# Helper loads in program order, two tile sets per phase for the kept sums, and a unit's additions written ahead of its low part

## The chip, the cores and the metric

The kernel runs on one core of one Trainium2 chip. The metric is the device time of one execution in microseconds (us). Before the change it is 2220.44 us, the median of three runs (2217.88 to 2223.58). The execution that the hardware profiler recorded took 2220.94 us.

## The reference, cut to what matters

Two residual layers on one sequence of 256 tokens with 2048 channels, all in float32. Layer 0 mixes tokens by attention in a neighbourhood of a grid, layer 1 by a short gated convolution; each is followed by a gated MLP of width 5632 with a three-tap convolution after its up-projection; a last RMS norm closes.

```python
for i in range(DEPTH):                                  # DEPTH = 2
    a = rms_norm(h, mix_norm[i])
    mixed = neighborhood_attention(a, ...) if i == 0 else short_conv_mixer(a, ...)
    h = h + mixed
    h = h + conv_glu_ffn(rms_norm(h, ffn_norm[i]), ...)  # dwconv3(W_up x)+b, silu(g)*u, W_down
return rms_norm(h, final_norm)
```

With 256 tokens every weight is used once, so the program is a stream of weights: some 486 MB are read from HBM, split, multiplied and forgotten.

## The kernel before, in words

**Two roundings of one weight.** Weights arrive in float32. A piece of 128 x 1024 (a *chunk*) is loaded into a tile `raw` by the SP queue (six such tiles in turn, `RAWS`). ScalarE (ACT in the profile) casts it to the matmul's format, `hi` (L179), and VectorE (DVE) subtracts to get what the cast lost, `lo` (L180). TensorE (PE) multiplies by both, so each chunk costs ACT one cast and DVE one subtraction beside the matmuls. `prep_to` emits loads, casts and subtractions; it runs `AHEAD` = 4 entries of the list of chunks ahead of the item whose matmuls are being emitted.

**Stages.** `Phase` computes a product whose result has channels on the partitions: query/key (four groups of heads), the short convolution's input (`wsc`), the MLP's up-projection (`wup`, each layer in two halves, here *up 00, 01, 10, 11*). An item is two output blocks of 128 channels: 4 chunks, 32 matmuls with `hi` (L251) and 32 with `lo` (L259). When an item's `lo` matmuls end, its results are taken out of PSUM: `corr` on ACT and on DVE (L304, L305), then for the MLP a multiplication into `pad` (L310), a convolution (L318 on ACT, twice L320 on DVE), a gate (L724, L727) and a split (L283 on ACT, L284 on DVE). For query and key it is L304, L305, L574, L283, L284, and then the scores (L596 to L598 on PE), the bias (L603), the maximum (L606), the exponential (L608), L609, L611, and transposes on PE (L621). `Values` computes the values after each query/key group. `Tokens` computes a product whose result has tokens on the partitions: `wo`, the MLP's down-projection (`wdown`, *down 00 to 11*) and `wscout`.

**Seven products in the place of eight.** In `Tokens` a plan (`S_MLP`, `S_ATT`, `S_OUT`) names pairs of blocks of inner channels; a pair marked H (a *kept unit*) is computed with seven block products, which need sums of weight blocks. Two of the sums are made early, by a *job*: `make` loads three 128 x 512 pieces into tiles of the pool of activations (`act`, SP queue, L192), adds on DVE (L198, L199) and stores two results to DRAM through the ACT queue (L204, tile `kept`). The jobs are spread over the phases that stand ahead of the stage that needs them (`QK_JOBS`, `V_JOBS`, `UP_JOBS`, `SC_JOBS`); in the list of chunks a job is an entry of its own, `"make"`, placed by `Phase.__init__` between items `lo` and `hi` of the phase. Its additions are emitted when four, and its stores when seven, further entries have been prepared. In the kept unit the stored sums come back as one `raw` (t13), are split, and two additions on DVE (L159, L160) make the two other sums (t24), which are split too.

**Who sets the order.** The program is written for a scheduler: instructions are emitted in the order of the code, the scheduler puts each on its engine's queue when it reckons its inputs to be there, and `tc.issue_after` keeps an instruction behind another. What comes out is a fixed list for each engine, worked off from the top: an instruction that waits holds up all behind it on its engine. The loads of a job's pieces stand behind the newest load (`newest["SP"]`), but the loads of chunks carry no such order among themselves or against the jobs.

Of the kernel before, what the change touches and what calls it, by code (L numbers as in the profile page):

```python
# [15 lines left out]
F32 = mybir.dt.float32  # L16
F32R = mybir.dt.float32r
# [5 lines left out]
P = 128  # L23
D = 2048
S = 256
KT = D // P
# [8 lines left out]
CH = 8  # L35
# [10 lines left out]
def plan(text, due):  # L46


    words = text.split()
    return (tuple(int(x[1:]) for x in words), {int(x[1:]) for x in words if x[0] == "H"}, due)  # L50
# [5 lines left out]
         (1, 0): S_FIRST, (1, 1): (plan("P0 P2 H1 H3 H4 P9 H6 H7 H8 P5 P10", 1), plan("P0 P2 H1 H3 P5 H4 H6 H7 P8 P9 P10", 0))}  # L56
S_OUT = (plan("P0 H1 H2 P3 H4 H5 H7 P6", 0), plan("P0 P3 H1 H2 H4 H5 H7 P6", 0))
S_ATT = (plan("P0 P1 P2 H6 P3 H7 P4 P5", 1),) * 2
QK_JOBS, V_JOBS, UP_JOBS, SC_JOBS = (0, 4, 4, 0), (2, 3, 2, 0), (9, 8, 11, 8), 16


HEAD = (2, 4)
# [9 lines left out]
C_END = C_ID + P  # L72

LEAD = 96
RAWS = 6


@with_exitstack
def trunk(ctx, tc, xT, par, bias, wqk, wv, wo, wsc, wscout, wup, wdown, out):
    nc = tc.nc  # L80
    cp = ctx.enter_context(tc.tile_pool(name="const", bufs=1))
    wp = ctx.enter_context(tc.tile_pool(name="wts", bufs=1))
# [8 lines left out]

    cp.tile([P, LEAD], F32, name="lead")
    pt = cp.tile([P, C_END], F32, name="pt")
# [31 lines left out]
    prepped = []  # L125

    stores = []

    def prep_to(n):
        while len(prepped) < min(n, len(chunks)):  # L130
            src, w, kind = chunks[len(prepped)]
            for due in [x for x in stores if x[0] <= len(prepped)]:
                stores.remove(due)
                due[1]()
            if kind == "make":
                make(*src)
                prepped.append(())
                continue
            raw = wp.tile([P, CH * P], F32, name="raw", tag="raw", bufs=RAWS)
            if kind == "rows":  # L140
                newest["SP"] = nc.sync.dma_start(out=raw[:, :w], in_=src)
                prepped.append(parts(raw[:, :w]) + (raw,))
                continue

            if kind == "kept":
                newest["SP"] = nc.sync.dma_start(out=raw, in_=src())
                t13 = parts(raw)
                prepped.append((t13, parts(pair_of_sums(raw, prepped[-1][2], prepped[-2][2]))))
                continue

            newest["SP"] = nc.sync.dma_start(out=raw[:, :4 * w].rearrange("p (f c) -> p f c", f=4),
                                             in_=src.rearrange("f p c -> p f c"))
            prepped.append(parts(raw[:, :4 * w].rearrange("p (f k c) -> p f k c", f=4, c=P)) + (raw,))

    def pair_of_sums(t13, w22, left):

        l = left.rearrange("p (f k c) -> p k f c", f=4, c=P)
        t2, t4 = w22[:, :4 * P], w22[:, 4 * P:].rearrange("p (f c) -> p f c", f=4)
        nc.vector.tensor_add(out=t2, in0=t13[:, :4 * P], in1=t2)  # L159
        nc.vector.tensor_add(out=t4, in0=t2.rearrange("p (f c) -> p f c", f=4), in1=l[:, 1])  # L160
        return w22

    def parts(r):

        if len(r.shape) == 4 and r.shape[2] == 1:
            y = wp.tile([P, CH * P], F32R, name="hi", tag="hi", bufs=6)
            hi, lo = y[:, :4 * P], y[:, 4 * P:]
            return split_parts(hi, lo, r)
        hi = wp.tile([P, CH * P], F32R, name="hi", tag="hi", bufs=6)
        lo = wp.tile([P, CH * P], F32R, name="lo", tag="lo", bufs=6)  # L170
        return split_parts(hi, lo, r)

    def split_parts(hi, lo, r):
# [5 lines left out]
        newest["ACT"] = nc.scalar.copy(out=hv, in_=r)  # L179
        newest["DVE"] = nc.vector.tensor_sub(out=lv, in0=r, in1=hv.bitcast(F32))  # L180
        return hi, lo

    kept, newest = {}, {}

    def make(w, g, i):

        kept[id(w), g, i] = dst = dp.tile([P, 8 * P], F32, name=f"kept{len(kept)}")
        tiles = [act_tile().bitcast(F32) for _ in range(3)]
        for x, f, k in zip(tiles, (0, 4, 4), (0, 0, 1)):
            f, k = 8 * g + f, 2 * i + k  # L190
            with tc.issue_after(newest["SP"].ins):
                nc.sync.dma_start(out=x.rearrange("p (f c) -> p f c", f=4),  # L192
                                  in_=w[f:f + 4, :, k * P:(k + 1) * P].rearrange("f p c -> p f c"))
        l, r, t = tiles

        def adds():
            with tc.issue_after(newest["DVE"].ins):
                nc.vector.tensor_add(out=l, in0=l, in1=r)  # L198
                nc.vector.tensor_add(out=t, in0=t, in1=r)  # L199

        def store():
            for n, x in enumerate((l, t)):
                with tc.issue_after(newest["ACT"].ins):
                    nc.scalar.dma_start(out=dst[:, n * 4 * P:(n + 1) * 4 * P], in_=x)  # L204
        stores.append((len(prepped) + 4, adds))
        stores.append((len(prepped) + 7, store))

    jobs = []

# [1 line left out]
        jobs.extend((w, g, i) for g, (order, sset, _) in enumerate(plans) for i in order if i in sset)  # L211

    def take(n):
        out, jobs[:] = jobs[:n], jobs[n:]
        return out

    class Phase:

        def __init__(self, w, fts, nk, src, evac, intro=0, step=CH, jobs=()):
# [73 lines left out]
    def act_tile():  # L295
        return ap_.tile([P, 2 * S], F32R, name="act", tag="act", bufs=HALF)
# [259 lines left out]
    a2 = [None] * KT  # L556
# [289 lines left out]
    Phase(wsc, range(3 * KT), KT, a2, sc_evac, intro=3, jobs=take(SC_JOBS))  # L846
    Tokens(wscout, KT, yT, to_norm(3, a3), S_OUT, yforms)
    mlp(1, a3, last_evac())

# [33 lines left out]
    for r in range(KT // STEP):  # L883
        for i in range(STEP // 2):
            k = r * STEP + 2 * i
# [97 lines left out]
```

## Time and profile before

| | |
|---|---|
| profiled execution | 2220.94 us, span 2219.1 us |
| granted TensorE clock, mean | 0.997 |
| busy time of PE / DVE / ACT | 2190.1 / 1853.0 / 1290.4 us |
| attention (query/key, values, scores) | 0 to 305 us |
| `wo` | 305 to 394 us |
| up 00, down 00 | 394 to 641, 641 to 755 us |
| up 01, down 01 | 755 to 998, 998 to 1118 us |
| short convolution's input, `wscout` | 1118 to 1392, 1392 to 1483 us |
| up 10, down 10 | 1483 to 1730, 1730 to 1847 us |
| up 11, down 11 and the end | 1847 to 2091, 2091 to 2219 us |

A row of the list of groups reads: line, engine, operation, written tile and read tiles, shapes, number; then busy time, mean nanoseconds of one, and the engine's idle time ahead of them with what ended most of it. A row of the timeline reads: start, length, engine, line, operation, tiles, number of instructions joined in the row, and in brackets the idle time ahead of it and its releaser. Matmuls are pipelined, so their cost is read from start to start.

### The profile page before, as it was taken

How to read it: one execution, taken by the hardware profiler on the slowest of the kernel's cores; microseconds unless marked ns; L12 is line 12 of the kernel's file. 1: busy time of each engine (PE TensorE's matmuls, PEld its weight loads, DVE VectorE, ACT ScalarE, POOL GpSimd, SP SyncE). 2: the span in 40 equal slices, each digit the busy share in tenths (PEclk: the TensorE clock that was granted, in tenths of full speed). 3: DMA queues.
4: the chain of work that ended last, by engine and by line, in shares of the span. 5: the costliest groups of instructions: out<-in, count | busy, mean ns of one | idle time of the engine just before them, and what ended most of it. 6: DMA issues, size and time to landing. Idle time of an engine off the chain costs nothing.

```text
span 2219.1 us, 33057 instructions
## 1 busy us (share of the span) xinstructions
PE 2190.1 (99%) x11710; PEld 1887.3 (85%) x11710; DVE 1853.0 (84%) x2856; ACT 1290.4 (58%) x1991; POOL 109.0 (5%) x159
## 2 busy tenths in 40 slices
PE   9999999999999999999999999999999999999998
PEld 8888888888888888887888888878888878888886
DVE  8788778888889888788887777888788989888888
ACT  7555555666665666565564455566556556566565
POOL 1011100000000000000000010000010000000000
PEclk9999999999999999999999999999999999999999
DMA  8799647777657788766698885677876667877575
GB/s 290 252 323 296 209 158 222 259 249 248 213 185 231 232 264 256 237 198 208 211 321 283 275 273 190 198 242 252 265 248 212 199 226 248 251 249 237 160 234 157
DMA packets 347670, 524.91 MB, mean 237 GB/s; under 512 B 19824, under 2 KB 250352, under 8 KB 347504
## 3 DMA queue, kind: packets, MB, share of 16 engines
q1 hardware_dynamic: 327120, 487.55, 68.9%
q10 hardware_dynamic: 20384, 35.24, 4.2%
q8 instruction: 92, 1.51, 0.3%
q14 instruction: 74, 0.61, 0.1%
HBM read 486.01 MB, written 36.70 MB: 236 GB/s over the span
## 4 chain that ended last, share of the span: by engine, by line
PE 73%; DVE 15%; issue 5%; ACT 3%; DMA 3%; SPq 0%; POOL 0%; ACTq 0%; DVEq 0%
PE mm L251 36%; PE mm L259 19%; DVE lo L180 7%; PE mm L444 3%; PE mm L443 3%; PE mm L442 3%; ACT hi L179 3%; DVE raw L160 1%; PE mm L668 1%; PE mm L670 1%; PE mm L669 1%; DVE raw L159 1%; DVE hi L180 1%; DMA act<-in_wdown 1%; DMA raw<-in_wup 1%
## 5 line engine op out<-in xcount | busy, mean ns | idle before, releaser
L180 DVE TENSOR_TENSOR lo<-raw,hi 128x1024 fp32r<-128x1024 f32 (+1 forms) x858 | 1020.3, 1214 | 121.4 <-ACT hi L179 70.7
L179 ACT CAST hi<-raw 128x1024 fp32r<-128x1024 f32 (+1 forms) x924 | 905.1, 1009 | 371.7 <-DVE raw L160 136.2
L251 PE MATMUL mm<-a,hi 128*128 128x512 f32 x4096 | 962.9, 391 | 2.0 <-DVE a L292 0.9
L251 PEld LDWEIGHTS mm<-a,hi 128*128 128x128 f32 x4096 | 759.7, 188 | 156.0 <-DVE a L292 2.2
L259 PEld LDWEIGHTS mm<-a,lo 128*128 128x128 f32 x4096 | 513.8, 192 | 14.2 <-DVE lo L180 2.4
L259 PE MATMUL mm<-a,lo 128*128 128x256 f32 x4096 | 519.9, 283 | 2.2 <-DVE lo L180 2.2
L442 PE MATMUL mm<-hi,act 128*128 128x512 f32 x624 | 245.0, 394 | 5.3 <-DVE h L339 2.1
L444 PE MATMUL mm<-hi,act 128*128 128x512 f32 x624 | 243.8, 391 | 0.0
L318 ACT ACTIVATE conv<-pad,pt 128x256 f32<-128x256 f32 x176 | 103.0, 599 | 207.7 <-DVE pad L310 199.5
L443 PE MATMUL mm<-lo,act 128*128 128x512 f32 x564 | 220.5, 391 | 0.0
L320 DVE SCALAR_TENSOR_TENSOR conv<-pad,pt,conv 128x256 f32<-128x256 f32 x384 | 178.3, 480 | 27.3 <-ACT conv L318 20.7
L304 ACT COPY corr<-mm 128x256 f32<-128x256 f32 x256 | 90.9, 370 | 159.6 <-PE mm L259 138.1
L442 PEld LDWEIGHTS mm<-hi,act 128*128 128x128 f32 x624 | 117.6, 188 | 33.2 <-ACT hi L179 5.0
L444 PEld LDWEIGHTS mm<-hi,act 128*128 128x128 f32 x624 | 117.4, 188 | 24.3
L443 PEld LDWEIGHTS mm<-lo,act 128*128 128x128 f32 x564 | 106.4, 189 | 22.1
L305 DVE TENSOR_TENSOR corr<-mm,corr 128x256 f32<-128x256 f32 x256 | 104.7, 417 | 10.4 <-ACT corr L304 10.2
L198 DVE TENSOR_TENSOR act<-act 128x512 f32<-128x512 f32 x66 | 45.9, 695 | 67.2 <-DMA act<-in_wdown 45.2
L284 DVE TENSOR_TENSOR act<-conv,act 128x256 fp32r<-128x256 f32 x88 | 40.1, 456 | 61.0 <-ACT act L283 61.0
L442 PE MATMUL mu<-hi,sf 128*128 128x512 f32 x186 | 73.5, 395 | 7.3 <-ACT hi L179 7.3
L443 PE MATMUL mu<-lo,sf 128*128 128x512 f32 x186 | 73.4, 395 | 1.1 <-DVE lo L180 1.1
L444 PE MATMUL mu<-hi,sf 128*128 128x512 f32 x186 | 72.5, 390 | 0.0
L310 DVE TENSOR_TENSOR pad<-corr,rstd 128x256 f32<-128x256 f32 x176 | 71.8, 419 | 0.1
(160 smaller groups left out, 1573.4 us busy)
## 6 DMA issues: line engine op xcount, KB each, us to landing
raw<-in_wup SPq DMA_DIRECT2D x352, 512.0 KB, 5.1
raw<-in_wdown SPq DMA_DIRECT2D x124, 512.0 KB, 4.4
raw<-in_wsc SPq DMA_DIRECT2D x96, 512.0 KB, 5.6
act<-in_wdown SPq DMA_DIRECT2D x156, 256.0 KB, 6.2
kept<-act ACTq DMA_DIRECT2D x132, 256.0 KB, 4.9
raw<-kept SPq DMA_DIRECT2D x66, 512.0 KB, 3.8
raw<-in_wqk SPq DMA_DIRECT2D x56, 512.0 KB, 5.6
raw<-in_wv SPq DMA_DIRECT2D x32, 512.0 KB, 4.8
```

The source lines that it names most:

```text
L179: newest["ACT"] = nc.scalar.copy(out=hv, in_=r)
L180: newest["DVE"] = nc.vector.tensor_sub(out=lv, in0=r, in1=hv.bitcast(F32))
L251: nc.tensor.matmul(self.ps[ft], lhsT=prepped[i][0][:, o:o + P], rhs=self.src[k], start=k == 0, stop=False)
L259: nc.tensor.matmul(self.ps[ft][:, S:], lhsT=prepped[i][1][:, o:o + P], rhs=self.src[k][:, :S], start=False, stop=k == self.nk - 1)
L304: nc.scalar.copy(out=corr, in_=ps[:, S:])
L305: nc.vector.tensor_add(out=corr, in0=ps[:, :S], in1=corr)
L310: nc.vector.tensor_mul(out=dst, in0=both(ps), in1=rstd)
L318: nc.scalar.activation(c, x[:, 1:S + 1], AF.Identity, scale=w[1], bias=b)
L320: nc.vector.scalar_tensor_tensor(out=c, in0=x[:, tap:tap + S], scalar=w[tap], in1=c, op0=ALU.mult, op1=ALU.add)
L442: nc.tensor.matmul(ps, lhsT=xh, rhs=wh, start=start, stop=False)
L443: nc.tensor.matmul(ps, lhsT=xh, rhs=wl, start=False, stop=False)
L444: nc.tensor.matmul(ps, lhsT=xl, rhs=wh, start=False, stop=stop)
```

## The change

1. **Loads in program order.** A new helper `load` puts each load of a chunk and of a job behind the newest one, so SP's queue has the loads in the order in which the code emits them.
2. **Two sets of tiles.** The jobs that a phase takes share a list `sets`: the first two jobs allocate three `act` tiles each, the later ones use these sets in turn. The additions are emitted one entry (`ADDS`) and the stores three entries (`STORES`) behind the job; it was four and seven.
3. **Additions ahead of the low part.** `high_part` returns the cast and a function for the subtraction; for a kept unit the two additions are emitted between them.
4. **Where jobs stand.** `V_JOBS` and `UP_JOBS` move one job; the first item after which a phase takes a job is item 0 (phases without a narrow beginning, `intro`) or a fifth of the way (with one), where it was an eighth of the way in every phase; the last is at 0.7 (0.9 for `wsc`), where it was 0.75.

```diff
-QK_JOBS, V_JOBS, UP_JOBS, SC_JOBS = (0, 4, 4, 0), (2, 3, 2, 0), (9, 8, 11, 8), 16
+QK_JOBS, V_JOBS, UP_JOBS, SC_JOBS = (0, 4, 4, 0), (2, 2, 2, 0), (9, 9, 11, 8), 16
...
+ADDS, STORES = 1, 3
...
             if kind == "kept":
-                newest["SP"] = nc.sync.dma_start(out=raw, in_=src())
-                t13 = parts(raw)
-                prepped.append((t13, parts(pair_of_sums(raw, prepped[-1][2], prepped[-2][2]))))
+                load(raw, src())
+                t13, low = high_part(raw)
+                t24 = pair_of_sums(raw, prepped[-1][2], prepped[-2][2])
+                low()
+                prepped.append((t13, parts(t24)))
...
+    def load(out, in_):
+
+        with ExitStack() as order:
+            if "SP" in newest:
+                order.enter_context(tc.issue_after(newest["SP"].ins))
+            newest["SP"] = nc.sync.dma_start(out=out, in_=in_)
...
-        tiles = [act_tile().bitcast(F32) for _ in range(3)]
+        if len(sets) < 2:
+            sets.append([act_tile().bitcast(F32) for _ in range(3)])
+        else:
+            sets.reverse()
+        tiles = sets[-1]
...
-            with tc.issue_after(newest["SP"].ins):
-                nc.sync.dma_start(out=x.rearrange("p (f c) -> p f c", f=4),
-                                  in_=w[f:f + 4, :, k * P:(k + 1) * P].rearrange("f p c -> p f c"))
+            load(x.rearrange("p (f c) -> p f c", f=4), w[f:f + 4, :, k * P:(k + 1) * P].rearrange("f p c -> p f c"))
...
-        stores.append((len(prepped) + 4, adds))
-        stores.append((len(prepped) + 7, store))
+        stores.append((len(prepped) + ADDS, adds))
+        stores.append((len(prepped) + STORES, store))
...
-            made, lo, hi = 0, len(order) // 8, len(order) * 3 // 4
+            made, lo, hi = 0, len(order) // 5 if intro else 0, int(len(order) * until)
```

**What moves on the queues.** The new file's lines are shifted: its L162, L189, L192, L266, L274, L298 and L319 are L141, L179, L180, L251, L259, L283 and L304 of the kernel before. The first place is the beginning of up 01. On SP before (`raw_7790` to `raw_7832` are the first item's chunks, `raw_7926` to `raw_7944` the second's, `raw_8049` the third's first):

```order
L141 DMA raw_7832<-in_wup 128x1024
L141 DMA raw_7926<-in_wup 128x1024
L141 DMA raw_7932<-in_wup 128x1024
L141 DMA raw_7938<-in_wup 128x1024
L141 DMA raw_7944<-in_wup 128x1024
L141 DMA raw_8049<-in_wup 128x1024
```

On SP now (`raw_7788` is the first item's last chunk, `raw_7891` the second's first, `raw_8025` the third's first, `act_7883` to `act_8019` the pieces of two jobs):

```order
L162 DMA raw_7788<-in_wup 128x1024
L162 DMA act_7883<-in_wdown 128x4x128
L162 DMA act_7884<-in_wdown 128x4x128
L162 DMA act_7885<-in_wdown 128x4x128
L162 DMA raw_7891<-in_wup 128x1024
L162 DMA raw_7897<-in_wup 128x1024
L162 DMA raw_7905<-in_wup 128x1024
L162 DMA raw_7911<-in_wup 128x1024
L162 DMA act_8017<-in_wdown 128x4x128
L162 DMA act_8018<-in_wdown 128x4x128
L162 DMA act_8019<-in_wdown 128x4x128
L162 DMA raw_8025<-in_wup 128x1024
```

On ACT before, at the same place (`corr_7888` and `corr_7914` begin the taking out of the first item):

```order
L179 CAST hi_7834<-raw_7832 128x1024
L179 CAST hi_7928<-raw_7926 128x1024
L179 CAST hi_7934<-raw_7932 128x1024
L179 CAST hi_7940<-raw_7938 128x1024
L179 CAST hi_7946<-raw_7944 128x1024
L179 CAST hi_8051<-raw_8049 128x1024
L179 CAST hi_8057<-raw_8055 128x1024
L304 COPY corr_7888<-mm_7838 128x256
L304 COPY corr_7914<-mm_7855 128x256
```

On ACT now (`corr_7844` to `act_7879` is the taking out of the first item, `hi_7893` the second item's first cast):

```order
L189 CAST hi_7790<-raw_7788 128x1024
L319 COPY corr_7844<-mm_7794 128x256
L333 ACTIVATE conv_7848<-pad0_83,pt_79 128x256
L319 COPY corr_7870<-mm_7811 128x256
L739 ACTIVATE g_7852<-conv_7848 128x256
L333 ACTIVATE conv_7874<-pad1_84,pt_79 128x256
L298 CAST act_7879<-conv_7874 128x256
L189 CAST hi_7893<-raw_7891 128x1024
L189 CAST hi_7899<-raw_7897 128x1024
L218 DMA kept23_7882<-act_7883 128x512
```

The two jobs' loads have moved ahead of the second and third items' chunks on SP, and on ACT all four casts of the second item have moved from ahead of the first item's taking out to behind it.

The second place is the second query/key group, on PE: `hi` and `lo` are an item's two kinds of matmuls, `sc` its scores, `tr` the transposes of its probabilities. Before:

```order
L259 MATMUL mm<-a,lo 128x256 x9
L251 MATMUL mm<-a,hi 128x512 x32
L259 MATMUL mm<-a,lo 128x256 x16
L596 MATMUL sc<-qk 128x256
L597 MATMUL sc<-qk 128x256
L598 MATMUL sc<-qk 128x256
```

Now:

```order
L274 MATMUL mm<-a,lo 128x256 x16
L611 MATMUL sc<-qk 128x256
L612 MATMUL sc<-qk 128x256
L613 MATMUL sc<-qk 128x256
L611 MATMUL sc<-qk 128x256
L612 MATMUL sc<-qk 128x256
L613 MATMUL sc<-qk 128x256
L636 MATMUL tr<-pt,s 128x128 x4
L266 MATMUL mm<-a,hi 128x512 x16
L274 MATMUL mm<-a,lo 128x256 x6
```

The second item's 32 `hi` matmuls and 16 of its `lo` matmuls, which stood between the first item's last `lo` matmul and its scores, now stand behind the scores and the transposes.

The third place is a kept unit of `wscout`, on DVE: the rows with `raw_14906` (before) and `raw_14810` (now) as the read tile are the stored sums' subtraction, the rows that write `raw_14901` and `raw_14805` are the two additions. Before:

```order
L180 TENSOR_TENSOR hi_14903<-raw_14901,hi_14903 128x512
L180 TENSOR_TENSOR lo_14909<-raw_14906,hi_14908 128x1024
L159 TENSOR_TENSOR raw_14901<-raw_14906,raw_14901 128x512
L160 TENSOR_TENSOR raw_14901<-raw_14901,raw_14874 128x512
L180 TENSOR_TENSOR lo_14915<-raw_14901,hi_14914 128x1024
```

Now:

```order
L192 TENSOR_TENSOR hi_14807<-raw_14805,hi_14807 128x512
L192 TENSOR_TENSOR lo_14813<-raw_14810,hi_14812 128x1024
L168 TENSOR_TENSOR raw_14805<-raw_14810,raw_14805 128x512
L169 TENSOR_TENSOR raw_14805<-raw_14805,raw_14778 128x512
L192 TENSOR_TENSOR lo_14819<-raw_14805,hi_14818 128x1024
```

Nothing has moved here: the scheduler takes the subtraction first as it did. Of the program's 66 kept units the first addition stands ahead of the subtraction in 36 before and in 38 now.

More of the change, by code (lines that the diff above doesn't have):

```diff
@@ L140, in prep_to @@
             if kind == "rows":
-                newest["SP"] = nc.sync.dma_start(out=raw[:, :w], in_=src)
+                load(raw[:, :w], src)
                 prepped.append(parts(raw[:, :w]) + (raw,))
@@ L145, in prep_to @@
             if kind == "kept":
-                newest["SP"] = nc.sync.dma_start(out=raw, in_=src())
-                t13 = parts(raw)
-                prepped.append((t13, parts(pair_of_sums(raw, prepped[-1][2], prepped[-2][2]))))
+                load(raw, src())
[3 more added lines that the diff above has]
+                prepped.append((t13, parts(t24)))
                 continue
-            newest["SP"] = nc.sync.dma_start(out=raw[:, :4 * w].rearrange("p (f c) -> p f c", f=4),
-                                             in_=src.rearrange("f p c -> p f c"))
+            load(raw[:, :4 * w].rearrange("p (f c) -> p f c", f=4), src.rearrange("f p c -> p f c"))
             prepped.append(parts(raw[:, :4 * w].rearrange("p (f k c) -> p f k c", f=4, c=P)) + (raw,))
+    def load(out, in_):
[3 more added lines that the diff above has]
+            newest["SP"] = nc.sync.dma_start(out=out, in_=in_)
     def pair_of_sums(t13, w22, left):
@@ L163, in parts, with high_part @@
     def parts(r):
-        if len(r.shape) == 4 and r.shape[2] == 1:
[L166 to L173, printed above, removed]
+        both, low = high_part(r)
+        low()
+        return both
+    def high_part(r):
+        hi = wp.tile([P, CH * P], F32R, name="hi", tag="hi", bufs=6)
+        if len(r.shape) == 4 and r.shape[2] == 1:
+            hi, lo = hi[:, :4 * P], hi[:, 4 * P:]
+        else:
+            lo = wp.tile([P, CH * P], F32R, name="lo", tag="lo", bufs=6)
         if len(r.shape) == 4:
@@ L179, in split_parts, with low, make @@
         newest["ACT"] = nc.scalar.copy(out=hv, in_=r)
-        newest["DVE"] = nc.vector.tensor_sub(out=lv, in0=r, in1=hv.bitcast(F32))
-        return hi, lo
+        def low():
+            newest["DVE"] = nc.vector.tensor_sub(out=lv, in0=r, in1=hv.bitcast(F32))
+        return (hi, lo), low
     kept, newest = {}, {}
-    def make(w, g, i):
+    def make(w, g, i, sets):
         kept[id(w), g, i] = dst = dp.tile([P, 8 * P], F32, name=f"kept{len(kept)}")
-        tiles = [act_tile().bitcast(F32) for _ in range(3)]
+        if len(sets) < 2:
+            sets.append([act_tile().bitcast(F32) for _ in range(3)])
+        else:
+            sets.reverse()
+        tiles = sets[-1]
         for x, f, k in zip(tiles, (0, 4, 4), (0, 0, 1)):
             f, k = 8 * g + f, 2 * i + k
-            with tc.issue_after(newest["SP"].ins):
-                nc.sync.dma_start(out=x.rearrange("p (f c) -> p f c", f=4),
-                                  in_=w[f:f + 4, :, k * P:(k + 1) * P].rearrange("f p c -> p f c"))
+            load(x.rearrange("p (f c) -> p f c", f=4), w[f:f + 4, :, k * P:(k + 1) * P].rearrange("f p c -> p f c"))
         l, r, t = tiles
@@ L213, in take, with __init__ @@
     def take(n):
-        out, jobs[:] = jobs[:n], jobs[n:]
+        sets = []
+        out, jobs[:] = [(*job, sets) for job in jobs[:n]], jobs[n:]
         return out
     class Phase:
-        def __init__(self, w, fts, nk, src, evac, intro=0, step=CH, jobs=()):
+        def __init__(self, w, fts, nk, src, evac, intro=0, step=CH, jobs=(), until=0.7):
             self.w, self.nk, self.src, self.evac = w, nk, src, evac
@@ L845, in trunk @@
     mlp(0, a1, to_norm(2, a2))
-    Phase(wsc, range(3 * KT), KT, a2, sc_evac, intro=3, jobs=take(SC_JOBS))
+    Phase(wsc, range(3 * KT), KT, a2, sc_evac, intro=3, jobs=take(SC_JOBS), until=0.9)
     Tokens(wscout, KT, yT, to_norm(3, a3), S_OUT, yforms)
```

## The prediction

> **What bounds the kernel now.** I read the page's busy times and chain first, then the table by stage.
>
> ```profile
> PE 2190.1 (99%) x11710; PEld 1887.3 (85%) x11710; DVE 1853.0 (84%) x2856; ACT 1290.4 (58%) x1991; POOL 109.0 (5%) x159
> PE 73%; DVE 15%; issue 5%; ACT 3%; DMA 3%; SPq 0%; POOL 0%; ACTq 0%; DVEq 0%
> core 0: us, PE busy (x) PEld busy (x) DVE busy (x) ACT busy (x) POOL busy (x), PEclk, DMA share, GB/s
> 641.00:755.00 114.00, 112.67 (x492) 91.47 (x491) 101.72 (x119) 66.32 (x77) 0.00 (x0) 1.00 0.70 227
> 755.00:998.00 243.00, 243.00 (x1401) 215.26 (x1400) 204.36 (x340) 145.47 (x233) 14.70 (x28) 1.00 0.75 239
> 998.00:1118.00 120.00, 115.59 (x511) 93.15 (x509) 107.82 (x132) 71.63 (x91) 0.00 (x0) 1.00 0.68 215
> 1392.00:1483.00 91.00, 85.64 (x371) 68.21 (x370) 81.98 (x105) 54.32 (x73) 2.36 (x3) 0.98 0.65 207
> 1730.00:1847.00 117.00, 113.39 (x491) 90.81 (x490) 105.25 (x124) 66.08 (x79) 0.00 (x0) 1.00 0.68 218
> ```
>
> PE is the bound: in up 01 (755 to 998) it is busy in all 243.00 us, so whatever idles PE in a phase is added to the time in full. Outside the end PE idles in the `Tokens` stages: 1.33 + 4.41 + 5.36 + 3.61 = 14.7 us in the four quoted. The timeline shows why in `wscout` (DVE), and the one stall in a phase (PE), with what follows it:
>
> ```profile
> 1458.03 0.69 DVE L159 TENSOR_TENSOR raw<-raw 128x512 f32<-128x512 f32 x1
> 1458.75 0.69 DVE L160 TENSOR_TENSOR raw<-raw 128x512 f32<-128x512 f32 x1
> 1460.63 2.36 DVE L180 TENSOR_TENSOR lo<-raw,hi 128x1024 fp32r<-128x1024 f32 x2 [1.19 <-ACT hi L179]
> 1278.26 2.01 PE L259 MATMUL mm<-a,lo 128*128 128x256 f32 x8 [2.17 <-DVE lo L180]
> 1278.00:1283.00 5.00, 4.75 (x18) 4.15 (x19) 4.96 (x8) 1.70 (x3) 0.00 (x0) 0.66 0.94 251
> ```
>
> DVE adds (L159, L160), waits 1.19 us for the cast of the sum, and PE waits behind it. At 1278.26 PE has idled 2.17 us, and then the granted clock is 0.66 over 5 us: 0.34 x 5 = 1.7 us lost after a gap of 2.17.
>
> **Loads and jobs at a phase's beginning: the main term.** What I need is what a pass costs and what the taking out of an item costs. From the timeline, PE and ACT at the beginning of up 01, and the hand-over from DVE to ACT:
>
> ```profile
> 754.48 6.96 PE L251 MATMUL mm<-a,hi 128*128 128x512 f32 x30
> 761.28 4.00 PE L259 MATMUL mm<-a,lo 128*128 128x256 f32 x32
> 765.11 3.14 PE L251 MATMUL mm<-a,hi 128*128 128x512 f32 x13
> 757.48 1.05 ACT L179 CAST hi<-raw 128x1024 fp32r<-128x1024 f32 x1 [0.75 <-DMA raw<-in_wup]
> 2199.48 0.68 DVE L339 TENSOR_TENSOR h<-mm,h 128x512 f32<-128x512 f32 x1
> 2200.20 0.63 ACT L342 ACTIVATE s<-h 128x512 f32<-128x512 f32 x1 [7.33 <-DVE h L339]
> ```
>
> Before, the second item's `hi` is cast at 757.48, while PE has 7.6 us of the first item left (to 765.11): hidden. One hand-over costs 2200.20 - 2199.48 - 0.68 = 0.04 us. In the new order ACT casts the second item's first chunk only behind the first item's taking out, and that begins when the first item's last `lo` matmul ends. PE has nothing between that matmul and the one which needs the cast. So PE idles for the whole chain, whose links are these groups:
>
> ```profile
> L304 ACT COPY corr<-mm 128x256 f32<-128x256 f32 x256 | 90.9, 370 | 159.6 <-PE mm L259 138.1 <-DVE corr L305 9.4 <-DVE act L198 6.9
> L305 DVE TENSOR_TENSOR corr<-mm,corr 128x256 f32<-128x256 f32 x256 | 104.7, 417 | 10.4 <-ACT corr L304 10.2
> L310 DVE TENSOR_TENSOR pad<-corr,rstd 128x256 f32<-128x256 f32 x176 | 71.8, 419 | 0.1
> L318 ACT ACTIVATE conv<-pad,pt 128x256 f32<-128x256 f32 x176 | 103.0, 599 | 207.7 <-DVE pad L310 199.5 <-DVE corr L305 7.8
> L320 DVE SCALAR_TENSOR_TENSOR conv<-pad,pt,conv 128x256 f32<-128x256 f32 x384 | 178.3, 480 | 27.3 <-ACT conv L318 20.7 <-ACT conv L316 3.6
> L727 DVE TENSOR_TENSOR conv<-conv,g 128x256 f32<-128x256 f32 x88 | 37.2, 423 | 5.2
> L283 ACT CAST act<-conv 128x256 fp32r<-128x256 f32 x88 | 35.3, 401 | 12.4 <-DVE conv L727 11.8
> ```
>
> Up 01 and up 11: 0.370 + 0.417 + 0.419 + 0.599 + 2 x 0.480 + 0.423 + 0.401 + 1.05 (the cast) = 4.64, with ten hand-overs 5.05 us. The order has this twice in each (second and third item, one job in front of each): 4 x 5.05 = 20.2 us. Up 00 and up 10: the cast stands behind the convolution on ACT, 0.370 + 0.417 + 0.419 + 0.599 + 1.05 + 0.2 = 3.06, once in each: 6.1 us. `wsc`: behind L304 alone, 1.5 us once. These casts were moved since the jobs' loads, which wait for activation tiles that the stage before is still reading, now stand on SP ahead of the chunks; a fixed list keeps the cast late even where the chunk lands early.
>
> In query/key groups two and three the first item is followed by two jobs, and the same thing reaches further: `hi` of the second item now stands behind the first item's exponential, the transposes ahead of it on PE.
>
> ```profile
> 96.73 7.44 PE L251 MATMUL mm<-a,hi 128*128 128x512 f32 x32
> 104.01 2.08 PE L259 MATMUL mm<-a,lo 128*128 128x256 f32 x16
> L574 DVE TENSOR_TENSOR qk<-corr,rstd 128x256 f32<-128x256 f32 x32 | 13.1, 415 | 0.0
> L283 ACT CAST qk<-qk 128x256 fp32r<-128x256 f32 x32 | 12.8, 403 | 16.3 <-DVE qk L574 16.2
> L284 DVE TENSOR_TENSOR qk<-qk 128x256 fp32r<-128x256 f32 x32 | 14.6, 461 | 1.9 <-ACT qk L283 1.9
> L603 DVE SCALAR_TENSOR_TENSOR s<-sc,bias 128x256 f32<-128x256 f32 x32 | 12.8, 414 | 0.0
> L199 DVE TENSOR_TENSOR act<-act 128x512 f32<-128x512 f32 x66 | 45.3, 687 | 2.7 <-DMA act<-in_wdown 2.2
> L606 DVE TENSOR_REDUCE m<-s 128x2 f32<-128x512 f32 x16 | 10.8, 675 | 0.0
> L608 ACT ACTIVATE s<-s,m 128x256 f32<-128x256 f32 x32 | 16.0, 501 | 7.1 <-DVE m L606 7.1
> kept<-act ACTq DMA_DIRECT2D x132, 256.0 KB, 4.9
> act<-in_wdown SPq DMA_DIRECT2D x156, 256.0 KB, 6.2
> L198 DVE TENSOR_TENSOR act<-act 128x512 f32<-128x512 f32 x66 | 45.9, 695 | 67.2 <-DMA act<-in_wdown 45.2 <-DMA act<-in_wscout 17.3 <-DMA act<-in_wo 4.8
> 1111.46 1.53 SPq L192 DMA_DIRECT2D act<-in_wscout  x3
> ```
>
> Before, 9.2 us of matmuls (96.73 to 105.92) covered the way to the scores. Now PE idles for 0.370 + 0.417 + 0.415 + 0.403 + 0.461 = 2.07 to the scores, and behind them for 2 x 0.414 + 0.687 (a job's addition that now stands on DVE between the two biases) + 0.675 + 2 x 0.501 + 1.05 = 4.24, with ten hand-overs 6.7 us. Then the third and fourth job use the first two sets again: their loads wait for stores that stand on ACT behind that late cast, and the third item's chunks and DVE's work wait behind those loads. From that cast's start to the end of the third item's first cast: 1.05 + 1.05 (the next chunk's cast, ahead of the second store) + 4.9 (store) + 6.2 (load) + 0.695 (addition) + 0.401 (a cast held by it) + 1.05 = 15.3, and three loads issued in front on SP at 1.53 / 3 = 0.51: 16.9 us. PE has 1.05 and then an item, 32 x 6.80 / 30 + 3.83 = 11.1 us. So a second gap of 4.7, say 5 us; 3 if store and load come 2 us sooner together, 7 if they come 2 us later. Sum for two groups: 2 x (6.7 + 5) = 23.4 us.
>
> **The clock.** Ten of these eleven gaps are 3 us and longer. The gap of 2.17 cost 1.7 us of clock afterwards, the shorter ones of `wscout` 0.02 x 91 = 1.8 us all together. I take 1.0 for each, 10 us, between 0 and 17. The Trainium skill ("TensorE: Matmul & The Clock Gate", Part 1: the HAM clock gate) halves the clock only after a whole idle window of some 3.4 us; by that rule the 3.06 us gaps would cost nothing of the kind, and the sum would be 2 us lower. The trace differs: 2.17 us of gap were enough at 1278.26.
>
> **Two sets, earlier additions and stores.** In the middle of a phase a set comes back after at least eight chunks, two items of 11.1 us, against 6.2 + 4.9 for load and store: hidden; without that cover it is the wait of the third job above. The stall at 1278.26 stems from additions on DVE that stood in the way of `lo`; the new spread over `wsc` moves them, so I take back its 2.2 + 1.7 us.
>
> **Additions ahead of the low part.** DVE's order shows the addition first in 38 of 66 units, before it was 36: the scheduler undoes it. Gain: at most two waits of 1.19; I take 1 us. The stores and the moved jobs cost nothing of their own (DVE and ACT have idle time in every phase, 243 - 204.36 and 243 - 145.47 in up 01).
>
> **The sum.** 20.2 + 6.1 + 1.5 + 23.4 + 10 - 3.9 - 1 = 56.3. The profiled execution took 2220.9, its median 2220.4: 2220.9 + 56.3 - 0.5 = 2276.7, say 2277 us.
>
> **The rivals.**
> - *The change does what it is written for* (faster): loads come early enough that the casts' place doesn't matter, and the additions go first. Its price is the idle time above: 14.7 in the four stages and 3.9 at 1278, so 2202 us. It decides if casts are taken as their chunks land, so that less than a third of the 51 us of new gaps is real. For it: DVE's wait of 1.19 sits just where the subtraction of 1.214 stands first. Against it: both orders. Chance 0.08.
> - *The gaps are partly given back*: while PE stands, loads and DVE run ahead, and the `Tokens` stage behind a phase starts with a lead that covers its waits, at most the 14.7 us: 2262 us. For it: DVE is at 204.36 of 243 in up 01, so it is the nearest to PE. Against it: the waits of 1.19 come back in every unit, from a chain inside it. Chance 0.14.
> - *Later jobs stall too* (slower still): DVE takes a job's additions one chunk behind its load, with `lo` of later chunks behind them. If each of the 53 jobs in up and `wsc` phases cost PE 0.5 us, it is 27 us more: 2303 us. For it: DVE waited 67.2 us for such loads already, four entries behind. Against it: hardly any of that reached PE. Chance 0.12.
> - *Nothing is felt*: gaps and gains cancel, 2220 us. Chance 0.05.
>
> **How the numbers follow.** Forecast 0.61. The bounds of the unknown sizes are -4 and +4 in attention, -10 and +7 in clock: 2263 to 2288. With the case of gaps given back, at the low ends of attention and clock (2262 - 14 = 2248) and without the short gaps of up 00, up 10 and `wsc` (7.6 us, so 2240), and half of the later jobs' case above, 2240 to 2300 holds about 0.8. About 0.3%, 6.7 us, can be told from no change: faster 0.08, same 0.05, slower 0.87.
>
> **What would show it.** Right: in the second and third query/key group two gaps each, PE released by ACT L189; gaps of 5 us twice at the beginning of up 01 and up 11, with the taking out on ACT in front of the cast, and half clock behind some; wscout's waits unchanged. Wrong: PE unbroken at 765 us, or waits for DVE's additions of jobs in the middle of phases.

## The result and the profile after

The changed kernel takes 2275.43 us, the median of four runs (2272.17 to 2277.63), the kernel before in the same session 2219.16 (2217.40 to 2223.58): a ratio of 1.0249, with a 95% interval of 1.0228 to 1.0271. The profiled execution took 2272.17 us, the shortest of the four; its span is 2270.4, 51.3 longer than before, while the medians lie 56.3 apart.

The page's busy times, and the group of the `hi` matmuls of the phases (L266 is L251 before, where its idle time was 2.0):

```profile
PE 2205.6 (97%) x11710; PEld 1897.5 (84%) x11710; DVE 1862.2 (82%) x2856; ACT 1305.4 (57%) x1991; POOL 97.1 (4%) x159
L266 PE MATMUL mm<-a,hi 128*128 128x512 f32 x4096 | 976.3, 394 | 30.1 <-ACT hi L189 28.8
```

The 51.3 us split in two with this row and the one of before. PE's idle time is 2270.4 - 2205.6 = 64.8, before 29.0: 35.8 us more. PE is busy 15.5 us longer with the same 11710 matmuls. Nearly all of that is clock: by the traces PE is busy for 33.8 us at a granted clock of 0.50, before for 6.8, and half of the difference is 13.5 us. And PE now waits 28.8 us for ACT's casts in the phases.

The stages, with the windows moved to where they now lie: attention, down 00, up 01, down 01, `wscout`, down 10, up 11:

```profile
core 0: us, PE busy (x) PEld busy (x) DVE busy (x) ACT busy (x) POOL busy (x), PEclk, DMA share, GB/s
0.00:327.00 327.00, 310.75 (x1697) 269.47 (x1698) 244.07 (x414) 175.47 (x340) 22.02 (x23) 0.97 0.73 244
666.00:780.00 114.00, 112.40 (x493) 91.31 (x492) 101.74 (x120) 65.36 (x76) 0.00 (x0) 1.00 0.71 224
780.00:1039.00 259.00, 248.60 (x1409) 219.21 (x1408) 210.12 (x346) 150.11 (x234) 14.38 (x28) 0.98 0.70 231
1039.00:1158.00 119.00, 116.51 (x507) 93.85 (x505) 104.93 (x128) 72.01 (x92) 0.00 (x0) 0.99 0.69 216
1430.00:1519.00 89.00, 84.28 (x371) 67.25 (x370) 80.62 (x103) 53.85 (x73) 2.36 (x3) 1.00 0.65 209
1770.00:1882.00 112.00, 110.70 (x483) 89.84 (x482) 100.03 (x118) 64.50 (x75) 0.00 (x0) 1.00 0.70 226
1883.00:2143.00 260.00, 249.60 (x1409) 220.01 (x1408) 207.07 (x338) 149.18 (x230) 12.41 (x24) 0.97 0.67 219
```

Attention is 22 us longer (305 before), up 01 and up 11 each 16 (243 and 244 before): together more than the whole 51.3; up 00, up 10 and `wsc` add and save a few us. The `Tokens` stages idle as they did or a little less.

The beginning of up 01, in order of time: the second item's loads on SP, PE, and ACT:

```profile
776.74 1.48 SPq L162 DMA_DIRECT2D act<-in_wdown  x3
778.27 4.46 SPq L162 DMA_DIRECT2D raw<-in_wup  x4
787.17 3.99 PE L274 MATMUL mm<-a,lo 128*128 128x256 f32 x32
789.29 0.37 ACT L319 COPY corr<-mm 128x256 f32<-128x256 f32 x1 [7.63 <-PE mm L274]
794.96 0.40 ACT L298 CAST act<-conv 128x256 fp32r<-128x256 f32 x1 [1.53 <-DVE conv L742]
795.27 1.99 ACT L189 CAST hi<-raw 128x1024 fp32r<-128x1024 f32 x2
796.36 6.87 PE L266 MATMUL mm<-a,hi 128*128 128x512 f32 x19 [5.20 <-ACT hi L189]
```

ACT stands idle for 7.63 us until 789.29, and the cast of a chunk whose load began at 778.27 comes at 795.27, directly behind the taking out of the item before. PE, whose 32 `lo` matmuls from 787.17 on are done at 791.0 at their pace of 0.12 us each, waits for it. The matmul comes 5.36 us later than at the usual pace, four times in all in up 01 and up 11; 3.11 us in up 00 and up 10 (behind the convolution), 1.57 us in `wsc` (behind L319).

### The profile page after: what moved, and what is told of

The parts are those of the page before. It is cut to its first block, busy times and chain, and to the rows that moved or that the text cites. A ratio compares the mean times of both kernels' runs of the same rounds, so it can differ in the third digit from the quotient of the medians.

```text
span 2270.4 us, 33031 instructions
## 1 busy us (share of the span) xinstructions
PE 2205.6 (97%) x11710; PEld 1897.5 (84%) x11710; DVE 1862.2 (82%) x2856; ACT 1305.4 (57%) x1991; POOL 97.1 (4%) x159
## 4 chain that ended last, share of the span: by engine, by line
PE 85%; DVE 8%; issue 3%; ACT 3%; DMA 1%; SPq 0%; ACTq 0%; DVEq 0%
PE mm L266 41%; PE mm L274 21%; PE mm L458 5%; PE mm L459 5%; PE mm L457 5%; DVE lo L192 3%; ACT hi L189 2%; PE mu L458 2%; PE mu L459 2%; PE mu L457 1%; PE mm L684 1%; PE mm L685 1%; PE mm L683 1%; DVE raw L169 1%; DVE hi L192 1%
## 5 line engine op out<-in xcount | busy, mean ns | idle before, releaser
L192 DVE TENSOR_TENSOR lo<-raw,hi 128x1024 fp32r<-128x1024 f32 (+1 forms) x858 | 1016.4, 1213 | 165.9 <-ACT hi L189 74.1
L189 ACT CAST hi<-raw 128x1024 fp32r<-128x1024 f32 (+1 forms) x924 | 907.8, 1010 | 344.7 <-DVE raw L169 120.7
L266 PE MATMUL mm<-a,hi 128*128 128x512 f32 x4096 | 976.3, 394 | 30.1 <-ACT hi L189 28.8
L266 PEld LDWEIGHTS mm<-a,hi 128*128 128x128 f32 x4096 | 766.9, 190 | 188.9 <-ACT hi L189 33.8
L274 PEld LDWEIGHTS mm<-a,lo 128*128 128x128 f32 x4096 | 513.7, 191 | 12.2
L274 PE MATMUL mm<-a,lo 128*128 128x256 f32 x4096 | 519.5, 283 | 0.0
L319 ACT COPY corr<-mm 128x256 f32<-128x256 f32 x256 | 95.1, 372 | 296.8 <-PE mm L274 292.6
L457 PEld LDWEIGHTS mm<-hi,act 128*128 128x128 f32 x624 | 117.6, 188 | 29.8 <-ACT hi L189 5.0
L523 POOL TENSOR_TENSOR s<-conv 128x128 f32<-128x128 f32 x27 | 14.8, 549 | 975.3 <-DVE conv L742 975.3
```

The costliest lines, as they stand in the source:

```text
L266: nc.tensor.matmul(self.ps[ft], lhsT=prepped[i][0][:, o:o + P], rhs=self.src[k], start=k == 0, stop=False)
L274: nc.tensor.matmul(self.ps[ft][:, S:], lhsT=prepped[i][1][:, o:o + P], rhs=self.src[k][:, :S], start=False, stop=k == self.nk - 1)
L319: nc.scalar.copy(out=corr, in_=ps[:, S:])
L457: nc.tensor.matmul(ps, lhsT=xh, rhs=wh, start=start, stop=False)
```

## The experiments

Parts of the change are made alone and in pairs first, then single costs are taken out.

**The order of the loads alone.** The kernel before, with every load behind the newest load:

```diff
-                newest["SP"] = nc.sync.dma_start(out=raw[:, :w], in_=src)
+                load(raw[:, :w], src)
...
-            with tc.issue_after(newest["SP"].ins):
-                nc.sync.dma_start(out=x.rearrange("p (f c) -> p f c", f=4),
...
+            load(x.rearrange("p (f c) -> p f c", f=4), w[f:f + 4, :, k * P:(k + 1) * P].rearrange("f p c -> p f c"))
```

> The kernel before with loads in program order and nothing else of the change. Theory A (a job's loads, which wait for activation tiles still in use, hold up the chunks' loads behind them on SP, and so the scheduler lists the next item's casts on ACT behind the item before's taking out): with the old way of taking three new tiles for each job, this hits nearly every job. The order lists some 40 casts directly behind a taking out, most with chains of about 5.4 us: 190 to 240 us slower than before with the clock, 2410 to 2460 us, and gaps of PE released by ACT's cast all through the up phases. Theory B (the earlier beginning of the jobs makes the gaps): the same time as before, 2212 to 2226. Theory C (two sets with early additions and stores make the gaps, as waits for stores and for DVE): the same time as before too.

Measured 2526.87 us, ratio 1.1376 (1.1358 to 1.1394), with the page's row, and the group:

```profile
PE 2277.9 (90%) x11710; PEld 1946.7 (77%) x11710; DVE 1881.5 (75%) x2856; ACT 1306.8 (52%) x1991; POOL 93.4 (4%) x159
```

```profile
L255 PE MATMUL mm<-a,hi 128*128 128x512 f32 x4096 | 1044.7, 414 | 212.0 <-ACT hi L185 210.3 <-DVE a L296 1.0 <-DVE h L343 0.6
```

The order of the loads alone costs 306 us, more than I expected: 210.3 us of waits for casts, in 41 places of over 1 us, and 2277.9 - 2190.1 = 87.8 us by which PE is busy longer. By the trace's clock 82 of these are half clock, some 2 us for each place, where the prediction had taken 1.0. It is the harmful part.

**The two sets alone.** The kernel before with `sets`, additions one and stores three entries behind:

```diff
-        tiles = [act_tile().bitcast(F32) for _ in range(3)]
+        if len(sets) < 2:
+            sets.append([act_tile().bitcast(F32) for _ in range(3)])
+        else:
+            sets.reverse()
+        tiles = sets[-1]
...
-        stores.append((len(prepped) + 4, adds))
-        stores.append((len(prepped) + 7, store))
+        stores.append((len(prepped) + 1, adds))
+        stores.append((len(prepped) + 3, store))
...
```

> The kernel before with the two sets of tiles, additions one entry and stores three entries behind the job, loads unordered as before. Theory A: no cast stands behind a taking out in the order, so no new gap: 2210 to 2225 us; DVE waits more for job loads without PE feeling it. Theory C (two sets and early additions make the gaps): most of the 56 us, 2250 to 2290.

Measured 2223.54 us, ratio 1.0009 (0.9998 to 1.0020): no cost and no gain that can be told, so theory C falls. The sets are not quite free in attention, though: the trace has gaps of 2.22, 1.73 and 3.61 us there ahead of transposes (at 120.41, 156.64 and 213.80), which the kernel before has not.

**The places alone.** The kernel before with the new numbers of jobs, their first place and `until`:

```diff
-            made, lo, hi = 0, len(order) // 8, len(order) * 3 // 4
+            made, lo, hi = 0, len(order) // 5 if intro else 0, int(len(order) * until)
...
```

> The kernel before with the new places of the jobs alone (numbers per phase, first job at item 0 or a fifth, last at 0.7 or 0.9). Theory A: no cast behind a taking out in the order, the stall at 1278 may move: 2210 to 2225 us. Theory B (the earlier beginning makes the gaps): gaps at the beginning of query/key groups two and three, up 01 and up 11, 2250 to 2280.

Measured 2218.38 us, ratio 0.9991 (0.9979 to 1.0003): no change. Theory B falls.

**All but the order of the loads.** The changed kernel with the chunks' loads unordered again:

```diff
-                load(raw[:, :w], src)
+                newest["SP"] = nc.sync.dma_start(out=raw[:, :w], in_=src)
...
```

> The changed kernel without the order among chunk loads (job loads behind the newest load, as before the change); two sets, early additions, places and the additions ahead of the low part stay. Theory A: all eleven gaps of the changed kernel vanish, and the clock loss with them: 2210 to 2222 us. Theories B or C: the gaps stay, 2260 to 2280.

Measured 2219.73 us, ratio 0.9994 (0.9984 to 1.0005). All of the change's cost hangs on the order of the loads; the gaps of the up phases and of `wsc` are gone, and in attention one of 1.90 us and three of 0.6 to 1.3 us are left.

**Loads and two sets.** The kernel before with both:

> The kernel before with loads in program order and the two sets of tiles, the old places of the jobs, no additions ahead. Theory A (the loads wait for tiles that are still read; sets that come back after eight chunks are free by then, fresh tiles are not): the 300 us of the order alone shrink to the jobs that take fresh tiles: four casts behind a taking out in the up phases, and the attention's; 2245 to 2265 us. If the order alone is what costs, whatever tiles it waits for: still above 2400 us.

Measured 2273.36 us, ratio 1.0236 (1.0221 to 1.0251). The sets, with their earlier additions and stores, take 253 of the 306 us away. That fits theory A, by which a set that comes back is free and a fresh tile is not; tiles and earlier stores were not taken apart. My number was too low: what is left is as much as the change's whole cost, gaps of 5.48, 7.11, 5.48 and 5.42 us in up 01 and up 11, 2.91 in `wsc`, those of attention, 3.24 at 73.8, and one of 2.83 in up 00 behind DVE. The gaps of 3.11 us in up 00 and up 10 are not among them, so the places decide where some gaps stand; to the total they add nothing that can be told.

**Order of the loads, jobs on another queue.** The changed kernel with the jobs' loads issued from GpSimd:

```diff
-            load(x.rearrange("p (f c) -> p f c", f=4), w[f:f + 4, :, k * P:(k + 1) * P].rearrange("f p c -> p f c"))
+            nc.gpsimd.dma_start(out=x.rearrange("p (f c) -> p f c", f=4), in_=w[f:f + 4, :, k * P:(k + 1) * P].rearrange("f p c -> p f c"))
```

> The changed kernel with the chunks' loads in program order on SP, but the jobs' loads issued from GpSimd's queue, so that no chunk's load stands behind a job's. Theory A: the order lists no cast behind a taking out any more, the gaps go: 2212 to 2226 us. If an order among the chunks' loads is bad in itself: 2250 us and more. GpSimd's own work in these stages (the sums of activations) could now wait behind a job's load; that would show as PE waiting in the token stages.

Measured 2221.39 us, ratio 1.0002 (0.9992 to 1.0012). PE idles 28.4 us in all, before 29.0, so GpSimd's own work did not hold it up. Chunks in program order cost nothing; jobs in one line with them do.

**Only ACT's list.** Is the chunk late, or only its cast listed late? The changed kernel, loads untouched, with three entries prepared ahead of the taking out at four items (`fill` holds the numbers of the items behind them), and the taking out behind their casts:

```diff
                 if kb == self.nk:
-                    self.evac(ft, self.ps.pop(ft))
+                    with ExitStack() as order:
+                        if item[0] - self.at + 1 in self.fill:
+                            prep_to(ends[item[0]] + 3)
+                            order.enter_context(tc.issue_after(newest["ACT"].ins))
+                        self.evac(ft, self.ps.pop(ft))
...
```

> The changed kernel with the loads just as they are, in program order, and only ACT's order moved at four places: the casts of the second and third item of up 01 and of the second and fourth of up 11 stand ahead of the taking out of the item before. Theory A1 (the list on ACT makes the gap; the chunk itself lands in time): the four gaps of 5.36 us go, with their half clock: 21 to 32 us less than the changed kernel, 2243 to 2254 us. Theory A2 (the chunk comes late, behind the job's loads on SP, and the list only follows): the gaps shrink little, 2265 to 2276 us, PE released by a cast that waits for its load.

Measured 2245.67 us, ratio 1.0110 (1.0095 to 1.0126), 29.8 us less than the changed kernel. PE and ACT at the same place, `corr` now being L324:

```profile
787.57 4.00 PE L275 MATMUL mm<-a,lo 128*128 128x256 f32 x32
791.40 7.44 PE L267 MATMUL mm<-a,hi 128*128 128x512 f32 x32
785.62 1.05 ACT L189 CAST hi<-raw 128x1024 fp32r<-128x1024 f32 x1 [3.57 <-DMA raw<-in_wup]
791.43 0.64 ACT L324 COPY corr<-mm 128x256 f32<-128x256 f32 x2
```

The chunk's cast runs at 785.62, as soon as it lands, 5.8 us before PE wants it, and PE goes from 787.57 to 791.40 and on without a break. The load was behind the job's loads in both kernels. None of the four gaps is left in the trace: 4 x 5.36 = 21.4 of the 29.8 us are the gaps, and the other 8.4 are about the clock behind them, as the next kernel shows. So the gap is the list's: theory A1.

**Useless work in the gaps.** The changed kernel with 20 more matmuls in each of these four gaps:

```diff
+                    if not n and item[0] - self.at in self.fill:
+                        with tc.issue_after(self.last.ins):
+                            for _ in range(20):
+                                nc.tensor.matmul(self.ps[ft], lhsT=self.src[0][:, :P], rhs=self.src[0], start=True,
+                                                 stop=True)
...
```

> The changed kernel with 20 more matmuls (512 columns, into the next item's tile, overwritten by it) in each of the four gaps at the beginning of up 01 and up 11: 4.5 us of useless work in place of idling. If what the two stages lost beyond their gaps is the half clock that follows a gap (15.6 and 16.5 us more against 10.7 each of gaps, so 10.7 us), it is 8 to 11 us faster than the changed kernel, 2264 to 2268 us, with granted clock 1.00 at these places. If it is something else (DVE or loads catching up), the time stays within 3 us.

Measured 2266.90 us, ratio 1.0206 (1.0191 to 1.0222), 8.5 us less than the changed kernel. The timeline of PE with the useless matmuls (L269), and the window behind the gap:

```profile
790.72 4.72 PE L269 MATMUL mm<-a 128*128 128x512 f32 x20
796.08 7.10 PE L272 MATMUL mm<-a,hi 128*128 128x512 f32 x30 [0.64 <-ACT hi L189]
```

```profile
797.00:801.00 4.00, 4.00 (x20) 3.29 (x19) 4.00 (x4) 2.00 (x2) 0.00 (x0) 1.00 0.88 290
```

The same window in the changed kernel, the one behind the second gap of up 01, and that behind the gap of 3.11 us in up 00:

```profile
797.00:801.00 4.00, 4.00 (x11) 3.13 (x10) 4.00 (x5) 2.25 (x3) 0.00 (x0) 0.50 0.73 264
816.00:820.00 4.00, 4.00 (x15) 3.13 (x14) 4.00 (x4) 3.78 (x5) 0.00 (x0) 0.71 0.79 260
445.00:449.00 4.00, 4.00 (x21) 3.39 (x20) 3.92 (x6) 3.30 (x6) 0.00 (x0) 1.00 0.65 183
```

The cast still comes when it came; only the clock is 1.00 where it was 0.50, with 20 matmuls in 4 us for 11. So about 2 us of the cost of each of these gaps is the clock behind it: 2.1 by the medians, 1.4 by the two profiled executions (spans of 2270.4 and 2264.8). The changed kernel's own trace agrees: behind the four gaps PE is busy at half clock for 4.8, 3.1, 4.4 and 5.3 us, which is 8.8 us lost. The second gap, as long as the others, cost less, since the clock was back at 818.3.

**Additions ahead of the low part, as written.** The third part alone on the kernel before:

```diff
-                t13 = parts(raw)
-                prepped.append((t13, parts(pair_of_sums(raw, prepped[-1][2], prepped[-2][2]))))
+                t13, low = high_part(raw)
+                t24 = pair_of_sums(raw, prepped[-1][2], prepped[-2][2])
+                low()
+                prepped.append((t13, parts(t24)))
...
```

> The kernel before with the third part alone, as the change writes it (additions emitted ahead of the low part, nothing holds the scheduler to it). DVE's order differs from before in a unit or two, so no effect is expected: 2215 to 2224 us. If the way it is written were enough, it would come to the 2202 us of the kernel in which the order is held.

Measured 2221.02 us, ratio 1.0003 (0.9994 to 1.0012): nothing.

**The same, held.** The subtraction is put behind the second addition, which `summed` holds:

```diff
-                low()
+                with tc.issue_after(summed[0].ins):
+                    low()
...
```

> The kernel before with the third part made to hold: the subtraction of a kept unit's sums is put behind its two additions on DVE in all 66 units. If the waits of 1.19 us in the token stages come from the subtraction standing first, PE's idle time there (14.7 us in four stages) falls by half or more: 2205 to 2214 us. If the way from the stored sums' load to the second sum's cast is bound otherwise, or the delayed low part now makes PE wait: 2216 to 2228 us.

Measured 2201.87 us, ratio 0.9912 (0.9895 to 0.9928), 19 us faster than before and 3 us better than the range. The page's row, DVE's timeline in `wscout`, the group of subtractions, and the first matmuls of a kept sum in the `Tokens` stages, before (L442) and now (L448):

```profile
PE 2181.0 (99%) x11710; PEld 1888.0 (86%) x11710; DVE 1859.4 (84%) x2856; ACT 1295.7 (59%) x1991; POOL 105.8 (5%) x159
```

```profile
1450.82 0.69 DVE L162 TENSOR_TENSOR raw<-raw 128x512 f32<-128x512 f32 x1
1451.54 0.69 DVE L163 TENSOR_TENSOR raw<-raw 128x512 f32<-128x512 f32 x1
1452.15 3.64 DVE L186 TENSOR_TENSOR lo<-raw,hi 128x1024 fp32r<-128x1024 f32 x3
```

```profile
L186 DVE TENSOR_TENSOR lo<-raw,hi 128x1024 fp32r<-128x1024 f32 (+1 forms) x858 | 1020.1, 1213 | 75.6 <-PE mm L265 46.2 <-ACT hi L183 24.9
L442 PE MATMUL mu<-hi,sf 128*128 128x512 f32 x186 | 73.5, 395 | 7.3 <-ACT hi L179 7.3
L448 PE MATMUL mu<-hi,sf 128*128 128x512 f32 x186 | 72.3, 390 | 0.3 <-ACT hi L183 0.3
```

Behind the additions DVE has the postponed subtraction to do while ACT casts the sum, so the wait of 1.19 us is gone; DVE's waits for casts fall from 70.7 to 24.9 us, PE's wait for the sums' casts from 7.3 to 0.3. PE's idle time falls from 29.0 to 19.9, in the four `Tokens` stages from 14.7 to 2.7. The other half of the gain is not idle time: PE is busy 9.1 us less, of which the granted clock explains 1.7 (half clock over 3.41 us once, before twice); where the rest comes from was not settled. The stall of `wsc` is still there, 2.73 us long, at 1270.

**Put together.** Held additions with the new places on the kernel before, and held additions on the changed kernel without the order of the loads:

> The kernel before with the new places of the jobs and the additions held ahead of the low part; loads and tiles as before. If the two add up (places: 2 us less, the stall at 1278 gone; additions held: 19 us less), 2196 to 2202 us. If the places only move the stall, 2201 to 2206.

Measured 2198.92 us, ratio 0.9907 (0.9891 to 0.9923).

> The changed kernel without the order among chunk loads and with the additions held ahead of the low part; two sets, early additions and stores and places stay. 2197 to 2203 us, if held additions are worth the same 19 us here; the same as the kernel with places and held additions within 4 us if the two sets neither cost nor bring anything.

Measured 2203.28 us, ratio 0.9923 (0.9911 to 0.9935). Both beat both kernels; their intervals and that of the held additions alone (2201.87) overlap, so the held additions carry all the gain that can be told. The second one missed its range by 0.3 us, and is 4.4 us above the first where at most 4 was expected. Its trace has the sets' gap in attention again, 3.49 us ahead of transposes at 210.13, where the first has 1.47; a cost of the sets of a few us is not ruled out.

## Why the prediction was right or wrong

The forecast of 2277 us was right: the main gaps came where and as they were forecast, and their sizes nearly so. Some other terms were off. Step by step:

- *Gaps at the beginnings of up phases*: 5.05, 3.06 and 1.5 us forecast, 5.36, 3.11 and 1.57 measured, in the phases named and as often as forecast. The kernel with ACT's list alone moved shows the cause, the one with loads ordered alone and the one with loads unordered alone show where it comes from.
- *First gap in attention*: 6.7 forecast, 1.98 before the scores and 4.21 behind them measured (4.34 in the third group). The size was right, the last link was not: PE was to be released by the second item's cast (ACT L189), but it is released by ACT's split L298 ahead of the scores and, behind them, by DVE's L626, which scales the probabilities for the transposes (rows below). The cast ends at 108.98, ahead of PE's reaching the matmul that needs it at 109.52, so the 1.05 us for it did not belong in the sum; L626, which did, was left out.
- *Second gap in attention*: 5 us each forecast, 0.5 and 0.1 measured. This step failed. PE, the job's loads and the third item's cast after the first gap:

```profile
103.41 0.38 PE L611 MATMUL sc<-qk 128*128 128x256 f32 x1 [1.82 <-ACT qk L298]
108.78 1.08 PE L636 MATMUL tr<-pt,s 128*128 128x128 f32 x4 [4.05 <-DVE s L626]
107.10 0.33 ACTq L218 DMA_DIRECT2D kept<-act  x1
107.95 1.03 ACT L189 CAST hi<-raw 128x1024 fp32r<-128x1024 f32 x1
109.48 4.73 SPq L162 DMA_DIRECT2D act<-in_wdown  x6
120.61 1.06 ACT L189 CAST hi<-raw 128x1024 fp32r<-128x1024 f32 x1
121.80 4.30 PE L266 MATMUL mm<-a,hi 128*128 128x512 f32 x16
```

 I had the stores begin behind two late casts and take 4.9 us. The first is issued at 107.10, ahead of the cast at 107.95, and the loads, which wait for stores, go out from 109.48 on, 2.4 us later. From the late cast's start to the end of the third item's first cast it is 121.67 - 107.95 = 13.7 us, not 16.9, and PE itself is slower in between by the half clock. This over-counted 9.4 us.
- *A gap I had not listed*: at the values of the first group PE waits 1.97 us. It is the rival of the later jobs, in a place I did not look at: a job's addition waits for its load, the split of the probabilities stands behind it on DVE, and the values' cast behind that on ACT:

```profile
70.58 0.69 DVE L213 TENSOR_TENSOR act<-act 128x512 f32<-128x512 f32 x1 [1.43 <-DMA act<-in_wo]
71.64 0.37 ACT L298 CAST act<-tr 128x256 fp32r<-128x256 f32 x1 [3.63 <-DVE act L299]
73.04 0.73 PE L683 MATMUL mm<-hi,a 128*128 128x512 f32 x2 [1.97 <-ACT hi L189]
```

 In the middle of the up phases and of `wsc`, where the rival had its price, there was no such wait.
- *The clock*: 10 us for ten gaps, with 1.7 taken back for 1278 (8.3), was too little, though the second gaps in attention did not come: PE is busy 15.5 us longer, 13.5 of it by the traces' clock. The four gaps that were filled gave back 8.5, so about 2 each and not 1.0. One price for every gap was the weak point: the gap of 3.11 us in up 00 cost no clock at all.
- *The stall at 1278*: gone, as taken back.
- *Additions ahead of the low part*: nothing, as read from the order; held by force they bring 19 us. The first rival's 14.7 + 3.9 comes near that by chance: of the 14.7 some 12 came, the stall of `wsc` stayed, and the rest is busy time that the rival did not price.
- *Gaps given back in the `Tokens` stages*: the four stages idle 1.60 + 2.49 + 4.72 + 1.30 = 10.1 us where it was 14.7. But in the kernel without the order of the loads, which has none of the phases' gaps, down 10 idles as little: PE is busy 112.23 of the stage's 113.57 us (1732.44 to 1846.01), here 112.27 of 113.57 (1769.70 to 1883.27). So there it is not the gaps that gave it back. What did is not settled.

So the errors nearly met: 9.4 us too many for the second gaps and 4.6 of idling less in the `Tokens` stages, against 15.5 - 8.3 = 7.2 too few for PE's longer busy time and 2.0 for the values' gap. What remains is about the 5 us by which the sum of 56.3 is above the profile's 51.3; that the medians, too, lie 56.3 apart is luck. So the right total is partly luck, the gaps of the phases and their cause are not.

## What to carry to other kernels

Putting loads in program order joins streams that were independent: a load that waits for a tile holds all behind it, and the scheduler then wrote the next item's casts behind the work before it, where they stay even if the data come in time. That it did so because it reckoned with the late load is read from the orders; no run shows it apart. So read the emitted order of each engine around every place where a tile can be late, and count what the bound engine has to do between the two instructions. An order that matters has to be held: written ahead, the additions stayed where they were in nearly all units; held with a dependency, they made the kernel 0.9% faster.

## What the runs showed of the hardware

A gap's cost on TensorE is not its length alone. Each of the four gaps of 5.36 us was followed by a granted clock of 0.50, for 3.1 to 5.3 us of PE's work, and filled gaps left it at 1.00. About three tenths of what the order of the loads cost was longer busy time of PE, nearly all of it clock (15.5 of 51.3 us, and 87.8 of 305.1 us by the spans, 2524.2 against 2219.1). The gap of 3.11 us in up 00 left the clock at 1.00, though the shorter one of 2.17 us at 1278 before the change had halved it, and so did one of 1.41 us in down 01 of the changed kernel (0.50 from 1091.4 to 1094.8). The same stall of `wsc` left it at 1.00 in the kernel with the additions only written ahead (2.23 us, up to 1277.57, then 26 matmuls in 5 us where it had been 18). So length alone did not decide. The Trainium skill ("TensorE: Matmul & The Clock Gate", Part 1: the HAM clock gate) has free-running windows of some 3.4 us, by which it depends on where a gap falls; its whole idle window, though, is more than 2.17 us of gap can hold, so the trace agrees with the windows (in the changed kernel the clock stays halved for 3.4, 6.8 or 10.2 us at a time) and not with that condition.
